# A hybrid decoder layer: gate tiles ahead of convolution tiles, and eight partial output products in the last recurrence

## The chip, the cores and the metric

The kernel runs on one core of a Trainium2 chip (trn2). The metric is the device time of one execution in microseconds (us); lower is better. The engines are called TensorE (PE in the profile; PEld is its weight load), VectorE (DVE), ScalarE (ACT), GpSimd (POOL) and SyncE (SP, which issues the transfers).

## The reference

One step of a one-layer decoder trunk. The input is 512 prompt tokens and 8 sequences of 8 sample tokens, 576 columns in all, of width 1024, in float32. With the two token mixers shortened to their names it reads:

```python
def token_mixers(hn, conv_buf, shift_buf, ssm0, wkv0, w):
    proj = hn @ w['w_in']
    z, xbc, dt_raw, rw = jnp.split(proj, IN_SPLITS, axis=-1)
...
    xbc_act = jax.nn.silu(conv)
    xs, bm, cm = jnp.split(xbc_act, XBC_SPLITS, axis=-1)
...
    y, ssm_fin = ssd_chunked(xs, dt, a_head, bm, cm,
...
    yg = (y.reshape(b, l, SSD_WIDTH) * jax.nn.silu(z.astype(f32))).reshape(b, l, SSD_GROUPS, SSD_WIDTH // SSD_GROUPS)
...
    o, wkv_fin = wkv_scan(rh, heads(decay), kh, vh, kk, heads(a), wkv0)
...
    y_rwkv = (on + bonus.reshape(b, l, RWKV_WIDTH)) * gate
    out = jnp.concatenate([y_ssd, y_rwkv], axis=-1).astype(dtype) @ w['w_out']

def layer(h, p, conv_buf, shift_buf, ssm0, wkv0, w):
    mix, conv_new, shift_new, ssm_new, wkv_new = token_mixers(
        rmsnorm(h, w['norm_mix']), conv_buf, shift_buf, ssm0, wkv0, w)
    h = h + mix
    hf = rmsnorm(h, w['norm_ffn'])
    h = h + (jax.nn.silu(hf @ w['w_gate']) * (hf @ w['w_up'])) @ w['w_down']
    gate = jax.nn.sigmoid(rmsnorm(h, w['norm_ple']) @ w['w_ple_gate'])
    h = h + gate * (p.astype(h.dtype) @ w['w_ple_proj'])
```

The combined projection gives 8 column tiles of 128 for the gate z, 12 for xBC (a causal convolution of 4 taps and SiLU follow), 16 columns of dt, and 26 tiles for RWKV-7 (r, k, v of 16 heads, and the low-rank inputs of decay, rate and gate). `ssd_chunked` is Mamba-2's recurrence in chunks of 128 tokens, `wkv_scan` the delta-rule recurrence of RWKV-7 with a 64x64 state for each head. The new states are outputs too.

## The kernel before

Activations lie transposed, channels on partitions and 576 token columns along them. A float32 product is made of three matmuls of split operands: high times high, high times low and low times high, each in two halves of 288 columns (`mm3`, L221 to L223). So a projection tile (1024 inputs, 128 outputs) is 48 matmuls. Each weight block of 128x512 is loaded by SP (`raw`), copied to its high part by ScalarE (`whi`) and its low part is made by VectorE and GpSimd in turns (`wlo`, L206); this is `wsplit`, called by `wload` and `linear` (L234). The blocks lie in one array in the order in which the program uses them.

**RWKV in quarters.** The 16 heads are worked in four quarters of four heads. Each needs six projection tiles with the token shift (`shifted`), then a preparation (`prep`: scan, exponentials, normalised keys; VectorE, ScalarE and GpSimd), the Gram matrices of nine windows of 64 tokens (`gram`, matmuls L613, masks L623), and the inverse of the triangular matrices: `solve`, some 60 small VectorE operations that follow each other (L667 to L677), and `combine`, which joins blocks on TensorE (L698, L712). Then comes `chain`: nine steps, one for each window, each of which needs the state of the one before. A step (`core` and what stands around it) has matmuls L789, a copy on VectorE (L792), matmuls L797, a second copy (L805), then the products for the state (L823) and four state updates on VectorE (L831). `head_norm` (L901, L902, L912) ends the quarter. The solves and chain steps leave TensorE idle unless other products fill it.

**The fill.** All projection tiles stand in one list, `todo`, made by `projections()`; `fill()` takes the first of it. A tile is of one of four kinds:

- the six of a quarter;
- a convolution tile (`conved`, "xbc"): after 48 matmuls ScalarE copies to `E`, GpSimd adds the old rows, VectorE does three multiply-adds of 128x600 (L395) and two products (L400, L401), and the result goes to memory;
- a gate tile (`zed`, "z"): two ScalarE operations and one on VectorE (L411, name `hz`), then to memory;
- `dts`, the 16 columns of dt.

The table `FP` tells how many tiles are taken at eight places of each quarter's preparation, gram and inverse, and `fill_for` takes tiles until the coming quarter has its six. The code's order is a wish only: the program is written within a TileContext that schedules all engines with a timeline model, so an instruction may go earlier or later on its engine. In the kernel before, the list is: six tiles of quarter 0; B and C of xBC (4 tiles) and dt; quarter 1; five X tiles; quarter 2; three X tiles; quarter 3; eight gate tiles.

**The last quarter.** After `chain(Q[3])` is written, the string `SEQ` orders what goes beside it, one letter for one thing: z is a gate tile, held back by `issue_after` to a marked matmul; s is the next step of the generator `ssd()` (Mamba's loads, decays, chunk states); p is the projection of the per-layer embedding (`ple_proj`); y loads the six RWKV output tiles of quarters 0 to 2; w is a partial output product, 36 matmuls over those six tiles, to which the layer's input is added and which goes to memory (`part_d`). `NPART` counts the w. After the head norm of quarter 3, the rest of `ssd()` is written (the loop over 8 sampled states, L1150 to L1167, and 8 pairs of heads, L1178 to L1205), and then eight residuals: output tile c takes two RWKV tiles (12 matmuls) and its partial sum when c is below `NPART`, else all eight (48 matmuls) and the layer's input. Line L1289 adds. Then come Mamba's part of the output product (`scaled`), the feed-forward part, the embedding gate and the last norm, which make up the time from 880 us on.

## Time and profile before

| | |
|---|---|
| time, median of 3 runs | 1346.01 us (1341.81 to 1350.75) |
| span of the profiled execution | 1349.0 us |
| mean granted TensorE clock | 0.940 |
| busy PE / DVE / ACT / POOL | 92% / 61% / 46% / 46% |
| moved | 135.58 MB, mean 100 GB/s |

The profile is of one execution; its span runs from the first to the last instruction. The busy share of an engine counts its instructions, not its waits; matmuls are pipelined and overlap, so that a busy TensorE may still be slowed, and the granted clock says at which share of its full speed it was let run. A table of windows gives, for a stretch of time, the busy time of each engine with the number of its instructions, the clock, the share of the transfer engines and the bytes moved. "A <- B" after an idle time is the engine and tile whose end released the waiting one.

### The profile page before, as it was taken

To read this page: it belongs to the slowest core of one execution; us is meant where nothing else is said; L and a number is where in the kernel's file an instruction comes from. 1 tells how busy PE (TensorE), PEld (TensorE's weight loads), DVE (VectorE), ACT (ScalarE), POOL (GpSimd) and SP (SyncE) were. 2 spreads that over 40 slices of the span, in tenths; PEclk is the share of its full clock that TensorE was granted. 3 is DMA by queue.
4 is the path that set the end of the run, shared out by engine and by line. 5 is a ranking of instruction groups with operands and counts; after the bars stand their busy time and mean duration, and the time that the engine had idled before them with its cause. 6 is when DMAs were issued, how large, how long until landed. Compare 5 with 4: busy or idle time off the path is not lost.

```text
span 1349.0 us, 26596 instructions
## 1 busy us (share of the span) xinstructions
PE 1246.8 (92%) x10525; PEld 1150.7 (85%) x10525; DVE 826.0 (61%) x1443; ACT 618.9 (46%) x1256; POOL 625.6 (46%) x597
## 2 busy tenths in 40 slices
PE   6897999999989978899999969989999999999997
PEld 6787897889868957788779859889999999999997
DVE  6648666887687785943466667886553135443454
ACT  6565436534654463343434364464442124433363
POOL 5425413642355154122456645565654336654642
PEclk9897799899979978889989989998999999999998
DMA  5322242234232412262454542222323222314322
GB/s 164 125 68 66 77 117 63 85 103 116 75 99 78 109 41 80 94 214 83 157 176 131 179 125 72 73 93 88 92 88 87 79 86 82 93 59 149 96 89 71
DMA packets 94461, 135.58 MB, mean 100 GB/s; under 512 B 34705, under 2 KB 39057, under 8 KB 94337
## 3 DMA queue, kind: packets, MB, share of 16 engines
q1 hardware_dynamic: 93760, 133.36, 32.4%
q8 instruction: 83, 1.36, 0.4%
q10 hardware_dynamic: 576, 0.52, 0.1%
q14 instruction: 42, 0.34, 0.1%
HBM read 106.10 MB, written 27.75 MB: 99 GB/s over the span
## 4 chain that ended last, share of the span: by engine, by line
PE 63%; DVE 14%; ACT 4%; issue 4%; DMA 3%; POOL 3%; DVEq 0%; SPq 0%; ACTq 0%; POOLq 0%
PE lin L234 21%; PE lin L1403 8%; PE lin L223 6%; PE lin L221 6%; PE lin L222 6%; DVE h L395 2%; PE lin L1508 1%; PE lin L1509 1%; PE lin L1510 1%; DVE tmp L674 1%; DVE wlo L206 1%; DVE Tt L676 1%; PE lin L613 1%; PE cx L797 1%; DVE suv L831 1%
## 5 line engine op out<-in xcount | busy, mean ns | idle before, releaser
L206 POOL TENSOR_TENSOR wlo<-raw,whi 128x512 fp32r<-128x512 f32 (+1 forms) x108 | 146.4, 1356 | 352.5 <-ACT whi L93 269.5
L93 ACT ACTIVATE whi<-raw 128x512 fp32r<-128x512 f32 (+1 forms) x232 | 143.3, 618 | 259.1 <-PE lin L234 126.4
L221 PE MATMUL lin<-xhi,whi 128*128 128x288 f32 (+1 forms) x784 | 243.3, 311 | 2.5 <-ACT whi L93 2.2
L223 PE MATMUL lin<-xhi,wlo 128*128 128x288 f32 (+1 forms) x784 | 241.5, 308 | 2.3 <-POOL wlo L206 2.3
L222 PE MATMUL lin<-xlo,whi 128*128 128x288 f32 (+1 forms) x784 | 241.5, 308 | 0.3 <-POOL xlo L194 0.3
L206 DVE TENSOR_TENSOR wlo<-raw,whi 128x512 fp32r<-128x512 f32 (+1 forms) x124 | 100.9, 814 | 103.2 <-PE lin L234 60.4
L221 PEld LDWEIGHTS lin<-xhi,whi 128*128 128x128 f32 (+1 forms) x784 | 151.0, 193 | 9.3 <-ACT whi L93 2.6
L223 PEld LDWEIGHTS lin<-xhi,wlo 128*128 128x128 f32 (+1 forms) x784 | 150.7, 192 | 6.2 <-POOL wlo L206 2.8
L222 PEld LDWEIGHTS lin<-xlo,whi 128*128 128x128 f32 (+1 forms) x784 | 150.8, 192 | 4.8 <-issue 1.2
L234 PE MATMUL lin<-xhi,whi 128*128 128x288 f32 x384 | 62.3, 297 | 3.2 <-ACT xhi L93 3.0
L234 PE MATMUL lin<-xlo,whi 128*128 128x288 f32 x384 | 60.8, 298 | 0.0
L234 PE MATMUL lin<-xhi,wlo 128*128 128x288 f32 x384 | 59.3, 297 | 0.0
L234 PEld LDWEIGHTS lin<-xhi,whi 128*128 128x128 f32 x384 | 54.6, 189 | 3.8 <-ACT xhi L93 1.7
L234 PEld LDWEIGHTS lin<-xlo,whi 128*128 128x128 f32 x384 | 54.8, 191 | 0.0
L234 PE MATMUL lin<-ah,wlo 128*128 128x288 f32 x352 | 54.7, 296 | 0.0
L234 PE MATMUL lin<-al,whi 128*128 128x288 f32 x352 | 54.7, 296 | 0.0
L234 PE MATMUL lin<-ah,whi 128*128 128x288 f32 x352 | 54.7, 296 | 0.0
L234 PEld LDWEIGHTS lin<-xhi,wlo 128*128 128x128 f32 x384 | 54.3, 191 | 0.0
L1403 PE MATMUL lin<-T,wh 128*128 128x288 f32 x320 | 50.1, 296 | 4.5 <-DVE T L194 2.8
L674 DVE TENSOR_TENSOR tmp<-L,Tt 72x30 f32<-72x30 f32 (+14 forms) x120 | 49.2, 410 | 3.2
L234 PEld LDWEIGHTS lin<-ah,whi 128*128 128x128 f32 x352 | 49.6, 189 | 0.0
L234 PEld LDWEIGHTS lin<-ah,wlo 128*128 128x128 f32 x352 | 49.6, 189 | 0.0
(425 smaller groups left out, 3197.8 us busy)
## 6 DMA issues: line engine op xcount, KB each, us to landing
raw<-wts SPq DMA_DIRECT2D x271, 256.0 KB, 2.6
S<-s_wkv SPq DMA_DIRECT2D x8, 512.0 KB, 5.1
hd<-s_ssm SPq DMA_DIRECT2D x8, 512.0 KB, 4.5
o_ssm_s<-hd SPq DMA_DIRECT2D x8, 512.0 KB, 2.9
xbc_d<-E SPq DMA_DIRECT2D x12, 288.0 KB, 2.1
x<-xT SPq DMA_DIRECT2D x8, 288.0 KB
gate_d<-g SPq DMA_DIRECT2D x8, 288.0 KB, 2.5
bv_d<-rw SPq DMA_DIRECT2D x8, 288.0 KB
```

The costliest lines, as they stand in the source:

```text
L93: return S.activation(out, in_, func, bias=bias, scale=scale)
L206: eng.tensor_tensor(lo[:, 0:n], raw[:, 0:n], hi[:, 0:n].bitcast(F32), ALU.subtract)
L221: T.matmul(ps[:, a:b], whi, xhi[:, a:b], start=first, stop=False)
L222: T.matmul(ps[:, a:b], whi, xlo[:, a:b], start=False, stop=False)
L223: T.matmul(ps[:, a:b], wlo, xhi[:, a:b], start=False, stop=last)
L234: T.matmul(ps[:, a:e], (hi, lo)[p][:, i * P:(i + 1) * P], xs[k + i][q][:, a:e], start=n == k + i == 0, stop=n == 2 and k + i == nk - 1, sk ...
L395: V.scalar_tensor_tensor(h[:], E[:, i:i + 600], w(i), h[:], ALU.mult, ALU.add)
L613: T.matmul(ps[:, c:c + 128].rearrange("p (a t) -> p a t", a=2), s.BK[jj][H[e], g].rearrange("p a t -> p (a t)"), s.G[H[e], g, jj, :, e], s ...
L674: V.tensor_tensor(o, L[:, jx:jx + 1, jx + 1:32].to_broadcast([NB, jx, n]), Tt[:, 0:jx, jx:jx + 1].to_broadcast([NB, jx, n]), ALU.mult)
L676: V.tensor_tensor(Tt[:, 0:jx, jx + 1:32], Tt[:, 0:jx, jx + 1:32], o, ALU.subtract)
L797: T.matmul(uw[H[e], jj, :], TT[H[e], g, jj, :], xs[H[e], jj, :], start=True, stop=True)
L1403: T.matmul(ps, (hi, lo)[p][:, k * P:(k + 1) * P], OPS[n][k][q], start=first and p == q == k == 0, stop=p == 1 and k == 3, skip_group_check ...
```

## The change

Five edits. `projections()` gives each of quarters 1 to 3 four convolution tiles right behind its own six tiles, and puts two "light" tiles (gate tiles, at the end one gate tile and dt) behind each quarter's; the list is then: six of quarter 0, z0, z1; six of quarter 1, B and C, z2, z3; six of quarter 2, X0 to X3, z4, dt; six of quarter 3, X4 to X7; z5, z6, z7. `FP` takes two tiles in each preparation instead of three, and `fill_for` goes on until no convolution tile heads the list, so that the four are written after the quarter's six and before its preparation. `SEQ` has no z: the embedding's projection comes first, and eight partial output products stand between and behind Mamba's steps, so `NPART` is 8 and every residual is the short one with 12 matmuls. The marks for the gate tiles go.

```diff
-SEQ = "zzszszszspyw"
+SEQ = "psyswswswwwwww"
...
-FILL = (5, 5, 3, 0)
-FP = ((1, 0, 1, 0, 1, 0, 0, 0), (1, 0, 1, 0, 1, 0, 0, 0), (1, 0, 1, 0, 1, 0, 0, 0), (0, 0, 0, 0, 0, 0, 0, 3))
+FP = ((1, 0, 1, 0, 0, 0, 0, 0), (1, 0, 1, 0, 0, 0, 0, 0), (1, 0, 1, 0, 0, 0, 0, 0), (0, 0, 0, 0, 0, 0, 0, 3))
...
-    rest = [("xbc", c) for c in CONV_BC] + [("dt", 0)] + [("xbc", c) for c in CONV_X] + [("z", c) for c in range(8)]
+    conv = [("xbc", c) for c in CONV_BC + CONV_X]
+    light = [("z", c) for c in range(5)] + [("dt", 0)]
     out = []
     for q in range(4):
         out += [(q, c) for c in in_tiles(q)]
-        out += rest[:FILL[q]]
-        rest = rest[FILL[q]:]
-    return out + rest
+        if q:
+            out += conv[:4]
+            conv = conv[4:]
+        out += light[:2]
+        light = light[2:]
+    return out + [("z", c) for c in range(5, 8)]
...
     def fill_for(s):
-        while len(s.t) < 6:
+        while len(s.t) < 6 or todo[0][0] == "xbc":
             fill()
...
-    while todo and todo[0][0] != "z":
-        fill()
+    assert all(what == "z" for what, _ in todo)
...
-    places = [("n", 2), ("c", 3), (3, 1), (3, 2), (3, 3)]
     for what in SEQ:
-        if what == "z":
-            with tc.issue_after(marks[places.pop(0)].ins):
-                fill()
-        elif what == "s":
+        if what == "s":
             next(steps)
```

What stands where is seen in the instruction order of each engine. The line numbers of the changed kernel are higher by 3 in its middle part and lower by 2 in the part from the SSD loop on.

VectorE in the preparation of the first quarter. Before (`h` and `E` are a convolution tile's, `kk`, `bk`, `lo`, `pb` the preparation's, `wlo` a weight split):

```order
L579 SCALAR_TENSOR_TENSOR kk_1131<-lo_1118,kk_1131 128x576
L395 SCALAR_TENSOR_TENSOR h_1087<-E_1079,hw,h_1087 128x600
L584 SCALAR_TENSOR_TENSOR bk_1145<-kk_1131,lo_1108 64x9x64 x2
L395 SCALAR_TENSOR_TENSOR h_1087<-E_1079,hw,h_1087 128x600
L581 TENSOR_TENSOR lo_1118<-lo_1118,rw_532 128x576
L395 SCALAR_TENSOR_TENSOR h_1087<-E_1079,hw,h_1087 128x600
L561 SCALAR_TENSOR_TENSOR lo_1245<-rmask,lo_1245 128x576
L206 TENSOR_TENSOR wlo_1297<-raw_1294,whi_1296 128x512
L400 SCALAR_TENSOR_TENSOR E_1079<-th_1092,h_1087 128x512
L401 SCALAR_TENSOR_TENSOR E_1079<-th_1092,h_1087 128x64
L565 TENSOR_TENSOR ar_981<-rw_834,pb_1258 128x576
```

And now (`hz` is a gate tile's):

```order
L579 TENSOR_TENSOR pb_1113<-kk_1123,pb_1113 128x576
L414 SCALAR_TENSOR_TENSOR hz_1083<-thz_1085,hz_1083 128x576
L582 SCALAR_TENSOR_TENSOR kk_1123<-lo_1110,kk_1123 128x576
L587 SCALAR_TENSOR_TENSOR bk_1137<-kk_1123,lo_1100 64x9x64 x2
L584 TENSOR_TENSOR lo_1110<-lo_1110,rw_539 128x576
L564 SCALAR_TENSOR_TENSOR lo_1222<-rmask,lo_1222 128x576
L209 TENSOR_TENSOR wlo_2031<-raw_2028,whi_2030 128x512
L568 TENSOR_TENSOR ar_988<-rw_841,pb_1235 128x576
L521 COPY rx_1246<-rn_1089 128x512
```

The convolution's multiply-adds between the preparation's steps are gone, and one operation of a gate tile stands in their place.

VectorE at the first chain steps of the third quarter. `TT` is the joined inverse, `xs` and `suv` are the two copies and the state updates of a chain step. Before:

```order
L719 COPY TT_465<-cx_5055 32x16x32
L581 TENSOR_TENSOR lo_6023<-lo_6023,rw_5621 128x576
L792 COPY xs_5111<-cx_5108 64x128
L561 SCALAR_TENSOR_TENSOR lo_6068<-rmask,lo_6068 128x576
L565 TENSOR_TENSOR ar_5968<-rw_5825,pb_6081 128x576
L805 TENSOR_SCALAR suv_5090<-cx_5114 64x2x64
L518 COPY rx_6092<-rn_6002 128x512
L595 SCALAR_TENSOR_TENSOR lo_6023<-rw_5757,pv,lo_6023 128x576
L831 SCALAR_TENSOR_TENSOR suv_5131<-suv_5090,pc_4410,cx_5126 64x64 x4
L574 SCALAR_TENSOR_TENSOR kk_6091<-rw_5689,pv,cb_6096 128x448
L792 COPY xs_5151<-cx_5148 64x128
```

And now:

```order
L722 COPY TT_472<-cx_5069 32x16x32
L795 COPY xs_5125<-cx_5122 64x128
L209 TENSOR_TENSOR wlo_6098<-raw_6095,whi_6097 128x512
L398 SCALAR_TENSOR_TENSOR h_6054<-E_6046,hw,h_6054 128x600
L808 TENSOR_SCALAR suv_5104<-cx_5128 64x2x64
L398 SCALAR_TENSOR_TENSOR h_6054<-E_6046,hw,h_6054 128x600 x2
L403 SCALAR_TENSOR_TENSOR E_6046<-th_6059,h_6054 128x512
L404 SCALAR_TENSOR_TENSOR E_6046<-th_6059,h_6054 128x64
L834 SCALAR_TENSOR_TENSOR suv_5145<-suv_5104,pc_4540,cx_5140 64x64 x4
L209 TENSOR_TENSOR wlo_6180<-raw_6177,whi_6179 128x512
L398 SCALAR_TENSOR_TENSOR h_6136<-E_6128,hw,h_6136 128x600
L795 COPY xs_5165<-cx_5162 64x128
```

What stood between the steps was the next quarter's preparation; now it is convolution tiles and weight splits, and that preparation comes later.

VectorE ahead of the SSD loop (`h` with the operand `lin` is a residual's add, `xdt` and `hin` are Mamba's chunk inputs and states). Before:

```order
L1289 TENSOR_TENSOR h_8706<-lin_8687,yl_8707 128x576
L206 TENSOR_TENSOR wlo_8744<-raw_8741,whi_8743 128x512
L1087 TENSOR_TENSOR xdt_7868<-d_7870,tk_7182 128x512
L1087 TENSOR_TENSOR xdt_7868<-d_7877,tk_7182 128x512
L1289 TENSOR_TENSOR h_8771<-lin_8710,yl_8772 128x576
L206 TENSOR_TENSOR wlo_8809<-raw_8806,whi_8808 128x512
L1102 TENSOR_TENSOR hin_7884<-hin_7884,d_7885 128x512
L1102 TENSOR_TENSOR hin_7884<-hin_7884,d_7889 128x512
L1087 TENSOR_TENSOR xdt_7893<-d_7895,tk_7182 64x512
L1087 TENSOR_TENSOR xdt_7893<-d_7902,tk_7182 64x512
L1289 TENSOR_TENSOR h_8836<-lin_8775,yl_8837 128x576
L206 TENSOR_TENSOR wlo_8874<-raw_8871,whi_8873 128x512
```

And now:

```order
L1287 TENSOR_TENSOR h_9084<-lin_9065,yl_9085 128x576
L1089 TENSOR_TENSOR xdt_8246<-d_8255,tk_7554 128x512
L1287 TENSOR_TENSOR h_9107<-lin_9088,yl_9108 128x576
L1287 TENSOR_TENSOR h_9130<-lin_9111,yl_9131 128x576
L209 TENSOR_TENSOR wlo_9161<-raw_9158,whi_9160 128x256
L1287 TENSOR_TENSOR h_9153<-lin_9134,yl_9154 128x576
L1104 TENSOR_TENSOR hin_8262<-hin_8262,d_8263 128x512
L1287 TENSOR_TENSOR h_9176<-lin_9157,yl_9177 128x576
L209 TENSOR_TENSOR wlo_9207<-raw_9204,whi_9206 128x256
L1104 TENSOR_TENSOR hin_8262<-hin_8262,d_8267 128x512
L1287 TENSOR_TENSOR h_9199<-lin_9180,yl_9200 128x576
L1089 TENSOR_TENSOR xdt_8271<-d_8273,tk_7554 64x512
```

The adds stood apart, each behind its own 48 matmuls and 128x512 splits, and five of the eight inside the loop's work; now all eight stand close together, each behind 12 matmuls and a 128x256 split.

## The prediction

> **What bounds the kernel now.** I read the page's head first, then busy time by stage, then durations of single forms, and last the waits in the stages that the change touches.
>
> ```profile
> span 1349.0 us, 26596 instructions
> PE 1246.8 (92%) x10525; PEld 1150.7 (85%) x10525; DVE 826.0 (61%) x1443; ACT 618.9 (46%) x1256; POOL 625.6 (46%) x597
> ```
>
> TensorE is busy for 92% of the span, so one would look for fewer matmuls. The change takes none away; it only puts them elsewhere. So what counts is where TensorE does not run at its rate. The next rows cut the span at the landmarks of the work: the end of gram of each quarter (139.5, 268.6, 409.2, 526.7), the first chain step of each quarter (201.3, 348.6, 485.0, 595.8), the first residual (697.3), the first sampled step of the SSD loop (722.0) and its end. The columns are: window, length, busy PE, PEld, DVE, ACT, POOL, granted clock, DMA share, GB/s. Two rows of the timeline show how such landmarks were found, the last block of gram and the first step of the chain.
>
> ```profile
> 137.30 2.08 PE L613 MATMUL lin<-G,bk 64*128 64x128 f32 x16 [0.52 <-ACT G L93]
> 201.32 0.71 PE L789 MATMUL cx<-suv,G 128*128 128x128 f32 x4
> ```
>
> ```profile
> 0.00:139.50 139.50, 110.73 (x814) 103.94 (x815) 89.58 (x134) 81.71 (x147) 63.07 (x95) 0.89 0.32 102
> 139.50:201.30 61.80, 58.61 (x509) 54.33 (x509) 43.04 (x97) 22.53 (x47) 18.43 (x19) 0.92 0.38 104
> 201.30:268.60 67.30, 62.02 (x577) 51.59 (x575) 48.43 (x86) 41.97 (x91) 33.90 (x45) 0.90 0.25 75
> 268.60:348.60 80.00, 77.51 (x783) 72.18 (x783) 60.66 (x140) 32.84 (x79) 26.99 (x31) 0.98 0.39 110
> 348.60:409.20 60.60, 55.12 (x501) 45.57 (x496) 49.51 (x82) 37.67 (x80) 31.22 (x42) 0.83 0.23 74
> 409.20:485.00 75.80, 69.49 (x712) 62.43 (x712) 58.14 (x141) 35.00 (x82) 23.77 (x26) 0.97 0.34 95
> 485.00:526.70 41.70, 33.01 (x335) 24.74 (x334) 28.25 (x56) 20.25 (x49) 20.56 (x23) 0.77 0.15 47
> 526.70:595.80 69.10, 60.84 (x571) 52.42 (x569) 48.39 (x120) 24.75 (x55) 17.09 (x20) 0.85 0.39 111
> 595.80:697.30 101.50, 96.97 (x808) 78.19 (x805) 46.75 (x106) 45.56 (x105) 38.41 (x33) 0.95 0.49 163
> 697.30:722.00 24.70, 24.70 (x196) 23.46 (x195) 16.61 (x25) 9.94 (x18) 13.19 (x11) 1.00 0.37 111
> 722.00:796.00 74.00, 68.05 (x658) 57.75 (x656) 46.37 (x90) 33.06 (x90) 46.25 (x40) 0.93 0.52 169
> 796.00:880.00 84.00, 74.75 (x650) 72.06 (x651) 61.21 (x66) 40.50 (x71) 46.29 (x27) 1.00 0.26 80
> 880.00:1349.00 469.00, 454.95 (x3444) 452.03 (x3442) 229.04 (x310) 193.10 (x348) 246.47 (x189) 0.98 0.29 88
> ```
>
> The reader is to see two kinds of stage. From 880 on, and from 697.3 to 722.0, TensorE is full at a clock near 1.00: nothing moves there but by its own count of matmuls. In the stages from a chain step to the end of gram (0.90, 0.83, 0.77) and in the first preparation TensorE is short of work, VectorE carries 70 to 85% of the time, and what is issued in between sets the end. There the DVE work that is added or removed is the price. The rate of TensorE with nothing in its way is this row:
>
> ```profile
> 1050.00:1100.00 50.00, 50.00 (x378) 50.00 (x377) 10.54 (x14) 10.79 (x18) 20.49 (x15) 1.00 0.28 81
> ```
>
> 50.0 / 378 = 0.132 us for a matmul of 128x288, so a projection tile of 48 matmuls is 6.35 us, a partial product of 36 is 4.8 us, and a residual of 12 is 1.6 us.
>
> **The change, part by part.** Prices on VectorE, one form in each row (busy, then mean ns):
>
> ```profile
> L395 DVE SCALAR_TENSOR_TENSOR h<-E,hw,h 128x600 f32<-128x600 f32 x36 | 36.7, 1018 | 4.7 <-ACT h L93 4.3
> L831 DVE SCALAR_TENSOR_TENSOR suv<-suv,pc,cx 64x64 f32<-64x64 f32 x112 | 31.3, 280 | 13.7 <-PE cx L823 11.2
> L400 DVE SCALAR_TENSOR_TENSOR E<-th,h 128x512 f32<-128x512 f32 x12 | 11.3, 939 | 0.0
> L805 DVE TENSOR_SCALAR suv<-cx 64x128 f32<-64x128 f32 x36 | 10.6, 294 | 14.0 <-ACT suv L93 13.1
> L792 DVE COPY xs<-cx 64x128 f32<-64x128 f32 x36 | 10.6, 294 | 15.4 <-ACT xs L93 14.8
> L401 DVE SCALAR_TENSOR_TENSOR E<-th,h 128x64 f32<-128x64 f32 x12 | 5.2, 435 | 0.0
> L411 DVE SCALAR_TENSOR_TENSOR hz<-thz,hz 128x576 f32<-128x576 f32 x8 | 6.1, 766 | 5.1 <-ACT thz L93 5.1
> ```
>
> A convolution tile costs VectorE 3 x 1.018 + 0.939 + 0.435 = 4.43 us, a gate tile 0.77, a chain step 0.294 + 0.294 + 4 x 0.280 = 1.71. On TensorE the two kinds of tile are alike. Now by stage, with counts from the instruction order before and after.
>
> *First preparation, to 139.5.* Three convolution tiles go, two gate tiles come: 3 x 4.43 - 2 x 0.77 = 11.8 us less on VectorE. Its own windows in the middle of it:
>
> ```profile
> 120.00:130.00 10.00, 5.76 (x76) 4.93 (x73) 9.74 (x11) 4.22 (x9) 6.98 (x8) 0.60 0.21 61
> 130.00:140.00 10.00, 7.91 (x60) 6.96 (x59) 4.92 (x12) 5.28 (x14) 8.28 (x15) 0.50 0.09 31
> ```
>
> VectorE is full until 130 and TensorE waits for it at half rate, so nearly all of it comes out: **-11** (bounds -5, if the ACT and POOL chain of gram then ends last, to -12).
>
> *First solve, to 201.3.* One convolution tile less among the solve's serial VectorE steps (4.43): **-3.5** (0, if projections on TensorE, 58.6 of 61.8 busy, end last, to -4.4).
>
> *First chain to second gram, 201.3 to 268.6.* One convolution tile, two gate tiles and one chain step more ahead of the last gram: 4.43 + 1.54 + 1.71 = +7.7 on a VectorE that has 67.3 - 48.4 = 18.9 us free. I take somewhat over half: **+4.5** (0 to +7.7).
>
> *Second solve to chain, 268.6 to 348.6.* Two convolution tiles and a chain step go from VectorE (10.6), and TensorE has about 6.3 projection tiles ahead of the matmuls that join the inverse instead of 8 (1.7 x 6.35 = 10.8). Both lie on the same stretch, so they don't add up wholly: **-14** (-8 to -18).
>
> *Second chain to third gram, 348.6 to 409.2.* One convolution tile, a gate tile, dt and three chain steps come in: 4.43 + 0.77 + 5.1 + about 1 = +11.5, and the stretch had 60.6 - 49.5 = 11.1 free. Since its VectorE mostly waits on steps that follow each other, little of it is free for a tile that stands between two steps: **+11** (+5 to +12). So the two stages together win 3 us: what the solve gives up, the chain gets.
>
> *Third gram to fourth gram, 409.2 to 526.7.* Here four convolution tiles come where none was ahead of gram: 4 x 4.43 = 17.7. Two chain steps more stand ahead of it (3.4). And the next preparation, of which a good part (18 us of VectorE by the order) was done before the first chain step at 485.0, now lies behind it: that shortens one stage and lengthens the next. Net +21 on VectorE against 41.7 - 28.3 = 13.4 free in the second of them. TensorE gets two more tiles of fill, 12.7 us, where its clock was 0.77, which hides them. I take **+18.5** (+8 to +25), nearer the full price since the order puts whole convolution tiles between a step's matmuls and its copies.
>
> *Fourth solve to chain, 526.7 to 595.8.* The head norm's VectorE copies move into the solve and three gate tiles stay; some 84 matmuls of the per-layer embedding (84 x 0.132 = 11 us) come ahead of the join, where the clock was 0.85 and TensorE 60.8 of 69.1 busy: they fit. **-5** (-8 to +3).
>
> *Last chain, 595.8 to 697.3.* Five gate tiles go (31.7 us), seven partial products come (33.6 us), the embedding goes before it. Seven more loads of 288 KB, as many stores, seven VectorE adds lie beside TensorE's 97 of 101.5 us and VectorE's 46.8. **-3** (-8 to +6, if the loads of x and of split weights come late).
>
> *Residual, 697.3 to 722.0.* All eight residuals, 12 matmuls each (12.7 us), stand together ahead of the loop; before, three stood here, one short and two of 48, among 196 matmuls. Each now reads 288 KB of partial sums, two buffers deep: **-3** (-8 to +4).
>
> *SSD loop, 722.0 to 796.0.* Residual tiles of 48 matmuls were its fill:
>
> ```profile
> L221 PE MATMUL lin<-xhi,whi 128*128 128x288 f32 x64 | 19.1, 299 | 0.0
> ```
>
> With the two other products that is 192 matmuls, four tiles, 25.3 us at 0.132. VectorE's waits there say what it costs to stand behind them:
>
> ```profile
> DVE yoff L1157 <- PE d L1153: 5.4, 5, 2.1
> DVE hd L1166 <- PE d L1165: 3.6, 4, 1.7
> DVE hd L1166 <- POOL hd L1161: 3.2, 5, 1.4
> DVE xs L1205 <- PE y L1204: 3.1, 3, 1.4
> DVE h L1289 <- PE lin L223: 2.6, 3, 1.5
> ```
>
> Waits on TensorE are 14.7 us; POOL's 3.2 stay. Each sampled state is loaded, updated and stored in one of two buffers:
>
> ```profile
> hd<-s_ssm SPq DMA_DIRECT2D x8, 512.0 KB, 4.5
> o_ssm_s<-hd SPq DMA_DIRECT2D x8, 512.0 KB, 2.9
> ```
>
> Load and store alone hold a buffer 7.4 us, 3.7 per state, and POOL's own 46 us are left, so the loop can't come below about 54. I take **-10** (-20 to 0).
>
> The rest of the program keeps its order: 0. The sum: -11 - 3.5 + 4.5 - 14 + 11 + 18.5 - 5 - 3 - 3 - 10 = **-15.5**. The profiled span of 1349.0 becomes 1333.5; it stands 3.0 us over the median of the runs shown (1346.01), so by the same ratio, 0.9978, the time is **1330.5 us**.
>
> **Rivals.** (1) *Chain steps that follow whole tiles, slower.* The interval between two chain steps is what TensorE has between them plus the round trip through VectorE:
>
> ```profile
> 290.30:305.00 14.70, 14.70 (x127) 13.77 (x126) 14.32 (x32) 5.92 (x12) 5.59 (x8) 1.00 0.26 77
> 510.00:515.50 5.50, 4.70 (x60) 3.60 (x59) 4.73 (x14) 3.21 (x11) 2.14 (x4) 1.00 0.27 101
> ```
>
> A step with little fill takes 5.5 us (second row); the stretch of the first row, 127 matmuls, has a full TensorE and a full VectorE at once. If a projection tile between two steps adds its matmuls (6.35) to its VectorE time, since the step's copies wait behind the one and its products behind the other, the first stage that begins with a chain step pays 7.7 + 6.35 = 14 where I had 4.5, the second 11.5 + 6.35 = 18 where I had 11, and the third 21 + 4 x 6.35 less the 41.7 x (1 - 0.77) = 9.6 us that TensorE's clock leaves free, 37 where I had 18.5. That is 35 us more: a sum of +19.5, 1368.5 in the trace, **1365 us**. For it: the clocks of 0.83 and 0.77 say that round trips, not TensorE's work, set these stages, and the changed order has convolution rows between a step's two copies. Against it: VectorE has 11 to 19 us free there. The kernel is slower than before once the three terms together pass 49.5 us (34 in my sum).
>
> (2) *The loop without fill gains nothing, no change.* TensorE's own work in the loop is 68.05 - 25.3 = 42.7 us at a clock of 0.93. Where TensorE was short of work its clock was 0.50 and 0.60 (the two rows of the first preparation). At 0.60 it is 42.7 x 0.93 / 0.60 = 66 us, and with the waits on POOL the loop stands at 72 or so; the residual stage likewise keeps its length. Then 13 of the 15.5 us are lost: 1346.5 in the trace, **1343.5 us**. For it: the loop's work comes in short pieces. Against it: 43 us of work in 60 is busier than those windows. [...]
>
> (3) *The free time of VectorE takes the convolutions, a larger gain.* With the two chain stages at +1 and +5 and the third at +10, the sum is -33: **1313 us**. For it: the 43 us that are free in the three stages together. Against: those are waits inside chains.
>
> (4) *That the change does not do it* can be left out: in the order printed for the changed kernel the gate tiles stand in the preparations, and eight short residuals together.
>
> **How the numbers follow.** My sum, 0.33, with (3) at 0.12 makes faster; (2), with the sum's own middling outcomes, 0.33; (1) 0.22. A measurement of this kernel tells about 1% from no change, that is 1332.5 and 1359.5; my forecast is barely over that bound, so much of its own spread falls into "same". Faster 0.45, same 0.33, slower 0.22. The range: the low end takes three terms at their better bounds (third to fourth gram +8, loop -20, last chain -8, that is 25 us less), 1305; the high end takes five sixths of what sets rival (1) apart from the sum, 1360.
>
> **What the changed profile would show.** The first gram should end near 128 instead of 139.5, with no L395-type work in 100 to 130. The stage from the third to the fourth gram should be 130 to 140 us instead of 117.5, the last chain of equal length, and the loop about 64 us between first sampled step and end, with VectorE's waits on TensorE nearly gone. Wrong would be: a clock near 0.6 in the loop with its length unchanged (rival 2), or growth over 49.5 us in the three stages from a chain step to gram (rival 1).

## The result and the profile after

The changed kernel takes 1394.79 us (median of 4 runs, 1392.91 to 1400.74) against 1343.91 us (4 runs, 1339.56 to 1350.75) for the kernel before on the same chips: a ratio of 1.0378, 95% interval 1.0338 to 1.0417. It is 51 us slower; the forecast was 1330.5 us, 15.5 us faster than the 1346.01 us known then. The head of its page shows no more work than before: as many matmuls (10525), and VectorE is busy for less time.

```profile
span 1391.0 us, 26671 instructions
PE 1273.4 (92%) x10525; PEld 1167.4 (84%) x10525; DVE 823.7 (59%) x1453; ACT 628.0 (45%) x1266; POOL 613.8 (44%) x601
```

The windows of the changed kernel, cut at the same landmarks as before (columns as there). The last three are cut otherwise than in the prediction, which ended the loop at 796.0, ahead of its last products: the loop up to the last products of the head pairs, the time from there to the first feed-forward product (the first that reads `XF`), and the rest:

```profile
0.00:129.80 129.80, 102.78 (x765) 95.34 (x765) 77.09 (x119) 76.67 (x137) 55.85 (x82) 0.89 0.33 105
129.80:187.30 57.50, 54.52 (x501) 52.21 (x501) 40.57 (x93) 17.64 (x42) 16.89 (x14) 0.94 0.39 105
187.30:270.00 82.70, 79.77 (x671) 66.90 (x667) 54.31 (x98) 50.57 (x106) 33.62 (x53) 0.88 0.25 82
270.00:335.80 65.80, 63.41 (x642) 59.48 (x640) 48.55 (x122) 25.09 (x61) 21.70 (x20) 0.97 0.41 108
335.80:424.50 88.70, 82.70 (x736) 68.13 (x732) 59.84 (x105) 55.68 (x113) 35.72 (x52) 0.85 0.25 78
424.50:491.50 67.00, 62.82 (x618) 58.75 (x616) 48.79 (x116) 24.38 (x58) 21.60 (x20) 0.95 0.36 99
491.50:570.70 79.20, 71.74 (x620) 58.61 (x616) 54.45 (x101) 46.69 (x97) 31.20 (x45) 0.78 0.25 75
570.70:642.20 71.50, 55.81 (x524) 49.12 (x522) 51.95 (x116) 25.19 (x51) 21.65 (x25) 0.90 0.50 141
642.20:748.10 105.90, 99.31 (x797) 80.40 (x797) 48.64 (x105) 37.44 (x93) 31.05 (x32) 0.89 0.47 149
748.10:773.50 25.40, 16.57 (x123) 14.65 (x123) 17.66 (x28) 8.95 (x17) 12.35 (x12) 0.89 0.53 158
773.50:854.50 81.00, 64.43 (x572) 50.49 (x572) 44.87 (x86) 37.58 (x100) 46.91 (x40) 0.74 0.36 121
854.50:904.90 50.40, 49.40 (x398) 48.32 (x399) 41.02 (x48) 21.40 (x38) 29.54 (x18) 1.00 0.23 74
904.90:1391.00 486.10, 470.15 (x3587) 465.04 (x3587) 235.99 (x319) 200.72 (x361) 255.74 (x195) 0.99 0.30 89
```

The kernel before, cut at the same landmarks (its feed-forward part begins at 862.3 us):

```profile
722.00:812.10 90.10, 79.55 (x783) 67.93 (x781) 56.87 (x102) 46.24 (x115) 53.77 (x45) 0.94 0.48 154
812.10:862.30 50.20, 47.20 (x383) 46.44 (x382) 40.56 (x45) 20.47 (x34) 30.75 (x19) 1.00 0.22 65
862.30:1349.00 486.70, 470.99 (x3587) 467.46 (x3587) 239.21 (x319) 199.95 (x360) 254.49 (x194) 0.98 0.29 89
```

The reader is to see the third, fifth and seventh rows: the stages from a chain step to the end of gram are 82.7, 88.7 and 79.2 us long where they were 67.3, 60.6 and 41.7. All of the loss stands before the first residual: 748.1 against 697.3 is 50.8 us. Some 9 us come back behind it, in the loop, which is 9 us shorter although its clock is 0.74 where it was 0.94; the two stretches after the loop are as long as they were. So the two traces are 42.0 us apart.

The same landmarks for the kernels that the next section speaks of, each from its profiled execution, in us from the stage's start to its end (loop and tail are the first two of the three windows above):

| stage | before | changed | list_only | parts_only | spread_conv | parts4 | spread_list |
|---|---|---|---|---|---|---|---|
| to gram 0 | 139.4 | 129.8 | 131.0 | 138.4 | 130.3 | 130.3 | 129.6 |
| solve 0 to chain 0 | 61.9 | 57.5 | 56.3 | 60.7 | 56.9 | 57.6 | 58.6 |
| chain 0 to gram 1 | 67.2 | 82.7 | 80.1 | 67.3 | 79.7 | 82.7 | 78.2 |
| solve 1 to chain 1 | 80.1 | 65.8 | 66.4 | 80.1 | 65.0 | 65.6 | 65.3 |
| chain 1 to gram 2 | 60.5 | 88.7 | 87.9 | 60.5 | 80.3 | 88.9 | 81.9 |
| solve 2 to chain 2 | 75.8 | 67.0 | 66.3 | 75.9 | 64.8 | 67.2 | 62.8 |
| chain 2 to gram 3 | 41.7 | 79.2 | 79.2 | 38.0 | 70.7 | 79.2 | 69.6 |
| solve 3 to chain 3 | 69.1 | 71.4 | 70.2 | 67.7 | 72.5 | 71.4 | 71.5 |
| chain 3 to residuals | 101.5 | 106.0 | 76.7 | 135.8 | 110.4 | 91.1 | 79.3 |
| residuals to loop | 24.7 | 25.3 | 26.7 | 19.7 | 25.1 | 23.1 | 27.7 |
| loop | 90.2 | 81.0 | 85.1 | 73.8 | 83.1 | 74.8 | 87.2 |
| tail | 50.1 | 50.4 | 50.5 | 52.2 | 48.6 | 51.8 | 50.7 |
| the rest | 486.8 | 486.0 | 483.3 | 483.1 | 487.1 | 485.4 | 483.1 |

The rest holds the same work in all of them and still runs from 483.1 to 487.1 us, and the stage from chain 2 to gram 3 is 41.7 or 38.0 us with the same list of tiles (before, parts_only): differences of 4 us between two traces say little.

What the three long stages gained is fill on TensorE. One row of each kernel, the third of the three matmuls of a split product, in the stage from chain 1 to gram 2, before:

```profile
L223 PE MATMUL lin<-xhi,wlo 128*128 128x288 f32 x43 | 13.1, 304 | 0.0
```

and changed:

```profile
L226 PE MATMUL lin<-xhi,wlo 128*128 128x288 f32 (+1 forms) x82 | 24.9, 303 | 0.0
```

Counted so over all split products, the three stages hold 185, 151 and 0 matmuls before and 266, 268 and 180 now; the two stages from gram to the chain that follow the first and the second hold 401 and 312 before and 332 and 324 now. At 0.132 us the additions are 10.7, 15.4 and 23.8 us; the stages grew by 15.4, 28.1 and 37.5, so the added matmuls alone don't make up the growth.

And where in the stage they stand (two windows of the changed kernel, one from the first chain step on and one at the end with gram; then the largest groups of TensorE in that end):

```profile
336.00:375.00 39.00, 39.00 (x337) 32.73 (x337) 26.91 (x40) 23.67 (x46) 17.33 (x24) 1.00 0.38 116
404.00:424.50 20.50, 20.50 (x200) 17.12 (x196) 10.70 (x26) 9.72 (x26) 9.96 (x15) 0.54 0.10 31
```

```profile
L616 PE MATMUL lin<-G,bk 64*128 64x128 f32 x64 | 8.6, 407 | 0.0
L737 PE MATMUL cb<-G,S 64*64 64x16 f32 x64 | 4.9, 266 | 0.0
```

First 39 us with a full TensorE at full clock, which hold two thirds of the stage's split products, and at the end 20.5 us at 0.54 with gram, the states and chain steps. The kernel before has such an end too,

```profile
391.00:409.20 18.20, 17.55 (x207) 15.07 (x206) 13.93 (x31) 10.59 (x27) 9.21 (x13) 0.61 0.05 18
```

so the low clock there is not new. In the stage from chain 2 to gram 3, which grew most, the changed kernel's parts are

```profile
491.50:530.00 38.50, 36.59 (x301) 30.62 (x297) 24.56 (x38) 23.39 (x45) 15.58 (x23) 1.00 0.38 112
530.00:550.00 20.00, 14.79 (x99) 10.71 (x100) 16.00 (x31) 14.01 (x28) 8.37 (x11) 0.55 0.14 50
550.00:570.70 20.70, 20.36 (x225) 17.29 (x223) 13.89 (x34) 9.28 (x25) 7.26 (x11) 0.61 0.10 29
```

The last two, 40.7 us, are about as long as the whole stage was (41.7). The projections stand in one heap ahead, and what they could have lain beside stands behind them.

### The profile page after: what moved, and what is told of

The parts are those of the page before. It is cut to its first block, busy times and chain, and to the rows that moved or that the text cites. A ratio compares the mean times of both kernels' runs of the same rounds, so it can differ in the third digit from the quotient of the medians.

```text
span 1391.0 us, 26671 instructions
## 1 busy us (share of the span) xinstructions
PE 1273.4 (92%) x10525; PEld 1167.4 (84%) x10525; DVE 823.7 (59%) x1453; ACT 628.0 (45%) x1266; POOL 613.8 (44%) x601
## 4 chain that ended last, share of the span: by engine, by line
PE 65%; DVE 16%; DMA 7%; ACT 5%; issue 4%; POOL 2%; SPq 0%; DVEq 0%; ACTq 0%; POOLq 0%
PE lin L237 21%; PE lin L1401 7%; PE lin L224 7%; PE lin L226 7%; PE lin L225 7%; PE lin L616 2%; DMA o_ssm_s<-hd 1%; DVE wlo L209 1%; PE cx L792 1%; DMA raw<-wts 1%; DVE tmp L677 1%; PE cx L800 1%; PE cx L815 1%; DMA yl<-part_d 1%; DVE Tt L679 1%
## 5 line engine op out<-in xcount | busy, mean ns | idle before, releaser
L224 PEld LDWEIGHTS lin<-xhi,whi 128*128 128x128 f32 (+1 forms) x784 | 149.2, 191 | 10.7 <-ACT whi L96 3.0
L237 PE MATMUL lin<-xhi,whi 128*128 128x288 f32 x384 | 60.5, 297 | 0.3 <-ACT xhi L96 0.2
L237 PE MATMUL lin<-xhi,wlo 128*128 128x288 f32 x384 | 60.6, 295 | 0.0
L1401 PE MATMUL lin<-T,wh 128*128 128x288 f32 x320 | 51.8, 299 | 5.3 <-ACT T L96 1.8
L1401 PEld LDWEIGHTS lin<-T,wh 128*128 128x128 f32 x320 | 45.4, 189 | 6.9 <-ACT T L96 2.3
L237 PEld LDWEIGHTS lin<-al,whi 128*128 128x128 f32 x352 | 49.7, 189 | 0.0
```

The source lines that it names most:

```text
L224: T.matmul(ps[:, a:b], whi, xhi[:, a:b], start=first, stop=False)
L237: T.matmul(ps[:, a:e], (hi, lo)[p][:, i * P:(i + 1) * P], xs[k + i][q][:, a:e], start=n == k + i == 0, stop=n == 2 and k + i == nk - 1, sk ...
L1401: T.matmul(ps, (hi, lo)[p][:, k * P:(k + 1) * P], OPS[n][k][q], start=first and p == q == k == 0, stop=p == 1 and k == 3, skip_group_check ...
```

## The experiments

Three theories for the loss, on record before the first four kernels ran: A, the matmuls of the convolution tiles ahead of gram; B, the partial products; C, the convolution's VectorE operations between the chain steps.

**The list alone.** The changed kernel with one partial product:

```diff
-SEQ = "psyswswswwwwww"
+SEQ = "sssspyw"
```

> The changed list of tiles and its fill rules, but with one partial output product as before (the residuals of 48 matmuls are back beside the SSD loop) and no gate tile in the last chain. Theory A (TensorE: the four convolution tiles behind each quarter's six stand ahead of gram as 25 us of matmuls, and what they leave is a starved end of the stage): the first chain step of the last quarter stays at about 642 us, the last chain shrinks from 106 to 75-80 us, the residuals and the loop take about what they took before (99); 1355-1365 us. Theory B (the partial products are what costs): back to 1345-1350. Theory C (VectorE's part of the convolution tiles costs): the last quarter's first step at 642 as in A, the total as in A.

Measured: 1363.15 us, ratio 1.0166 (1.0124 to 1.0208). The last chain took 76.7 us, as A and C said; B alone falls.

**The products alone.** The kernel before with eight partial products behind its gate tiles:

```diff
-SEQ = "zzszszszspyw"
+SEQ = "zzszszszspywwwwwwww"
```

> The list of tiles before, with eight partial products in the last chain behind the five gate tiles. All theories: first step of the last chain at about 596 as before. Theory A and C: the last chain, already full on TensorE, grows by the 33 us of the seven products, and the loop without its fill gives back 5 to 10 of them, with a clock near 0.75: 1365-1375 us. Theory B: about what the change measured, 1385-1395. If the loop gave back in full what it loses in fill: 1345.

Measured: 1365.00 us, ratio 1.0185 (1.0133 to 1.0236). The last chain grew by 34.3 us, seven products at their full 4.8, and residuals, loop and tail together fell from 165.0 to 145.7, by 19.3; theories A and C had 5 to 10. The loop without its fill took 73.8 us at a clock of 0.79. So by the ratios the list costs 22 us (0.0166 x 1343) and the products 25 (18 to 32), and 22 + 25 = 47 of the 51: the change has two losses that add up. In the traces these stages show 15 of the 25; the profiled run was this kernel's fastest, 1355.31 us.

**VectorE's part of the convolution.** The changed kernel without taps 1 to 3:

```diff
-        for i in range(1, 4):
-            V.scalar_tensor_tensor(h[:], E[:, i:i + 600], w(i), h[:], ALU.mult, ALU.add)
```

> The changed kernel without the three multiply-adds on VectorE in each of the twelve convolution tiles (36.7 us of VectorE in all; the convolution's taps 1 to 3 are left out). Theory A: TensorE's matmuls ahead of gram set the stages, so 5 to 12 us are won: 1383-1390. Theory C: these operations between the chain steps are what lengthens the three stages, 25 to 35 us are won: 1360-1370.

Measured: 1394.85 us, ratio 1.0383 (1.0329 to 1.0436): nothing is won by taking 36.7 us off VectorE. The stage from chain 1 to gram 2 has VectorE at 44.5 us instead of 59.8 and is as long as it was (88.5 against 88.7):

```profile
336.10:424.60 88.50, 83.97 (x738) 69.48 (x734) 44.49 (x92) 55.19 (x112) 32.75 (x53) 0.85 0.24 78
```

C falls.

**TensorE's part.** The changed kernel with half of each convolution tile's matmuls:

```diff
+                if part == 0 or i < part:
+                    mm3(ps, hi[:, i * P:(i + 1) * P], lo[:, i * P:(i + 1) * P], xh, xl, k + i == 0,
+                        k + i == (nk - 1 if part == 0 else nk - 5 + part))
...
-        linear(X, ps)
+        linear(X, ps, part=2)
...
```

> The changed kernel with 24 instead of 48 matmuls in each of the twelve convolution tiles (the second two inputs of each weight block are left out; loads and splits stay): 12 x 24 x 0.132 = 38 us less on TensorE. Theory A: the stages from a chain step to gram end 8 to 12 us earlier each, 25-35 us in all: 1360-1370. Theory C: TensorE has slack there, under 10 us are won: 1385-1392.

Measured: 1375.71 us, ratio 1.0271 (1.0217 to 1.0324); 0.0107 x 1343 = 14 us less than the changed kernel for 38 us of matmuls, with intervals that leave 5 to 23. The same stage is 9.2 us shorter (79.5). TensorE's part counts and VectorE's does not, but A's 25 to 35 were too much: more than half of what is taken away only leaves a gap.

**The place.** The same tiles in the same quarters, but taken one by one inside the preparation:

```diff
-FP = ((1, 0, 1, 0, 0, 0, 0, 0), (1, 0, 1, 0, 0, 0, 0, 0), (1, 0, 1, 0, 0, 0, 0, 0), (0, 0, 0, 0, 0, 0, 0, 3))
+FP = ((1, 0, 1, 0, 0, 0, 0, 0), (2, 1, 1, 1, 1, 0, 0, 0), (2, 1, 1, 1, 1, 0, 0, 0), (2, 1, 1, 0, 0, 0, 0, 3))
...
-        while len(s.t) < 6 or todo[0][0] == "xbc":
+        while len(s.t) < 6:
```

> The changed kernel with the same tiles in the same quarters, but the four convolution tiles and the two light ones taken one by one within the preparation (fill table rows 2 1 1 1 1) instead of four ahead of it. Theory A1 (the place: what stands ahead of the preparation delays it, and the preparation and gram then run with an empty TensorE at half clock): gram of quarters 1 to 3 ends 8 to 15 us earlier each, 20-35 us won in all, 1358-1375 us. Theory A2 (the amount: five gate tiles and the embedding are simply more TensorE work than these stages can hide): under 8 us won, 1385-1395.

Measured: 1371.71 us, ratio 1.0205 (1.0164 to 1.0247), 0.0173 x 1343 = 23 us won. The three stages hold 288, 288 and 192 matmuls of split products, more than the changed kernel's 266, 268 and 180, and are shorter by 3.0, 8.4 and 8.5 us. The stage from chain 1 to gram 2 and its end, which had a clock of 0.54:

```profile
331.90:412.20 80.30, 76.32 (x703) 63.74 (x698) 55.59 (x97) 48.87 (x103) 34.76 (x50) 0.91 0.25 79
...
392.00:412.20 20.20, 19.72 (x244) 15.46 (x242) 9.81 (x25) 11.49 (x28) 10.44 (x15) 0.83 0.13 43
```

So A holds in its narrower form A1: the place, four tiles in a heap ahead of the preparation, costs some 23 us. The tiles themselves are still paid where they stand now: the three stages hold 103, 137 and 192 more matmuls of split products than before, 13.6, 18.1 and 25.3 us at 0.132, and are 12.5, 19.8 and 29.0 us longer than before. The place was not tried by itself on the old list: the kernel before with its convolution tiles written ahead of the preparation (before_ahead, expected at 1353 to 1363 us if the place costs by itself) deadlocks and gave no time.

**Both losses undone.** spread_conv with one partial product, so that of the change only the new order of the tiles stays, gate tiles early and convolution tiles later:

```diff
-SEQ = "psyswswswwwwww"
+SEQ = "sssspyw"
```

> The changed list with the convolution tiles taken one by one in the preparations, and one partial product: both costly parts of the change undone, what stays is gate tiles ahead of convolution tiles. If the parts add up (list +22, of which place 22, products +24): 1335-1347 us, as before. If gate tiles in the early quarters cost by themselves (more TensorE work in stages with a half clock): 1350-1360.

Measured: 1348.18 us, ratio 1.0036 (1.0016 to 1.0057). Place and products make up 46 of the 51 us; the new order by itself costs some 5 (2 to 8), although the first chain step comes 13 us earlier (188.3 against 201.3).

**How many products.** The changed kernel with four:

```diff
-SEQ = "psyswswswwwwww"
+SEQ = "psyswswsww"
```

> The changed kernel with four partial products in the last chain instead of eight; four residuals of 48 matmuls stand by the SSD loop again. If each product costs the same (24 us for seven): 1378-1384 us. If the loop's gaps hold only the first few tiles: 1371-1376. If the products cost only beyond four, 1370 or less.

Measured: 1370.14 us, ratio 1.0194 (1.0158 to 1.0231). The first three products cost 0.0028 x 1343 = 4 us over list_only, the last four 0.0184 x 1343 = 25. From the first step of the last chain to the first feed-forward product, list_only, parts4 and the changed kernel do the same matmuls in another order (the products in the chain or in the residuals). Their rows, in this order, are

```profile
637.50:876.40 238.90, 220.10 (x1886) 188.16 (x1885) 150.04 (x255) 105.48 (x242) 124.29 (x97) 0.91 0.37 123
```

```profile
642.90:883.60 240.70, 219.87 (x1887) 187.18 (x1885) 150.33 (x260) 104.48 (x243) 121.92 (x98) 0.91 0.40 130
```

```profile
642.20:904.90 262.70, 229.71 (x1885) 193.86 (x1885) 152.19 (x266) 105.38 (x247) 119.86 (x100) 0.87 0.40 127
```

So the first three products cost 1.8 us and the last four 22.0, near the ratios' 4 and 25. The chain takes 14.4 us more for the first three, their full price, and 14.9 more for the last four. Behind the chain the first three win 12.7 us back; with the last four it is 7.2 us longer again, although 144 matmuls fewer stand there. The loop alone had clocks of 0.92, 0.89 and 0.74 (the last is in the windows of the changed kernel above):

```profile
740.80:825.90 85.10, 77.90 (x756) 66.92 (x752) 53.23 (x97) 44.11 (x112) 51.50 (x43) 0.92 0.45 152
```

```profile
757.10:831.90 74.80, 66.14 (x648) 54.47 (x647) 48.83 (x92) 40.18 (x105) 48.90 (x41) 0.89 0.48 160
```

Missing fill alone does not make the 81.0 us, since the loop of parts_only has none either and takes 73.8. Why the loop grows with the last four is not shown.

**Fill for the empty loop.** The changed kernel with 24 matmuls that no one reads in each sampled step, paced by that step's mask `bm`:

```diff
+        jk = mt("jk", [P, 8])
...
+            jp = lin_ps()
+            for i in range(24):
+                T.matmul(jp[:, 0:256], YR[7][0][:, 0:P], bm[:, i % 2], start=True, stop=True)
+            V.tensor_copy(jk[:], jp[:, 0:8])
```

> The changed kernel with 24 more matmuls of 128x256 (about 2.8 us) in each of the eight sampled steps of the SSD loop, whose result no one reads: about 22 us of TensorE work in place of the residual tiles' 25. Theory L1 (clock: without fill TensorE is held at 0.74, and its short matmuls then set the pace): the clock in the loop goes to 0.9 or more and the 81 us of the loop shrink to 70-77 although work was added. Theory L2 (transfers, POOL and waits set the pace): the work goes into gaps, 79-84 us at whatever clock. Theory L3 (TensorE's time adds up): 90-105 us.

Measured: 1387.60 us, ratio 1.0330 (1.0288 to 1.0371), not slower than the changed kernel's 1.0338 to 1.0417 and perhaps faster. Seven of the eight residuals moved into the loop's end as well, so its length can't be set against 81.0; from the last chain's first step to the first feed-forward product it is 257.1 against 262.7 us. The loop ran at 0.93:

```profile
761.90:848.40 86.50, 82.64 (x822) 72.17 (x822) 55.87 (x108) 44.30 (x114) 52.02 (x44) 0.93 0.45 154
```

The eight sampled steps alone can be compared. They hold 144 of the 192 added matmuls (48 went ahead of the first step) and one residual's 12. First the changed kernel, then this one:

```profile
773.50:826.80 53.30, 40.70 (x416) 31.22 (x415) 27.10 (x66) 19.24 (x55) 32.04 (x30) 0.76 0.37 129
761.90:814.00 52.10, 51.24 (x563) 44.49 (x562) 28.70 (x72) 17.49 (x51) 30.09 (x28) 0.92 0.36 133
```

L3 falls: the 192 matmuls are some 22 us (an estimate, 192 x 0.132 x 256 / 288), and the 144 of them that stand in these steps cost nothing there (52.1 against 53.3 us). The steps are as long at a clock of 0.92 as at 0.76, which speaks for L2 and its gaps: TensorE's idle time went from 12.6 to 0.9 us, and in the changed kernel its largest wait there was for the loads of the states (7.3 us). L1 is not excluded, since the added work may have used up what the higher clock gave.

**Fill for the end of gram.** The changed kernel with 12 matmuls behind each of gram's five groups in quarters 1 to 3:

```diff
+            if s.q:
+                with tc.issue_after(gm.ins):
+                    jp = cb_ps()
+                    for i in range(12):
+                        T.matmul(jp[:, 0:HALF], X[0][0][:, 0:P], X[1][0][:, 0:HALF], start=True, stop=True)
+                    V.tensor_copy(jk[:], jp[:, 0:8])
...
```

> The changed kernel with 12 more matmuls of 128x288, whose result no one reads, behind each of the five groups of gram in quarters 1 to 3: 180 matmuls, 23.8 us of TensorE at its full rate, into a stretch where TensorE is busy all the time at a clock of 0.50 to 0.56. Theory G1 (half clock: gram's and the states' small matmuls fill TensorE's time but do not lift its clock, large ones do): the clock there rises to 0.8 or more and the extra work is paid back, 1385-1402 us against 1395. Theory G2 (TensorE's time adds up): 1412-1420.

Measured: 1398.45 us, ratio 1.0405 (1.0368 to 1.0442): 4 us more than the changed kernel for 23.8 us of work, with intervals that overlap, within G1's numbers. But the clock at the end of gram rose only to 0.68 in the stage from chain 1,

```profile
400.00:427.00 27.00, 25.48 (x221) 21.63 (x223) 12.23 (x31) 12.86 (x32) 10.48 (x19) 0.68 0.08 24
```

and in the stage from chain 2 it was 0.62 (545.0 to 576.0) where it had been 0.61. The three stages grew by 4.1, 6.3 and 8.3 us. Of these 18.7 us 6.3 came back in the two solves that follow and 3.3 in the last chain, so G1's reason is hardly borne out.

**A tile in gram.** The kernel before with each preparation's third convolution tile held until gram's third group:

```diff
-FP = ((1, 0, 1, 0, 1, 0, 0, 0), (1, 0, 1, 0, 1, 0, 0, 0), (1, 0, 1, 0, 1, 0, 0, 0), (0, 0, 0, 0, 0, 0, 0, 3))
+FP = ((1, 0, 1, 0, 0, 0, 1, 0), (1, 0, 1, 0, 0, 0, 1, 0), (1, 0, 1, 0, 0, 0, 1, 0), (0, 0, 0, 0, 0, 0, 0, 3))
...
+                with tc.issue_after(pin[0]) if pin[0] else nullcontext():
+                    mm3(ps, hi[:, i * P:(i + 1) * P], lo[:, i * P:(i + 1) * P], xh, xl, k + i == 0, k + i == nk - 1)
...
+                pin[0] = gm.ins
                 fill_at(s, 5 if gs[0] == 0 else 6)
+                pin[0] = None
```

> The kernel before with the third convolution tile of each preparation of quarters 0 to 2 held back until the matmuls of gram's third group and put between them and the fourth. Theory G1: the 48 matmuls lift the clock in gram and come out of the full stretch ahead, 1 to 3 us a quarter: 1333-1340 us against 1342.5. Theory G2: 6.35 us are moved from one place to another of the same stage, and the chain steps that follow wait: 1342-1350.

Measured: 1369.47 us, ratio 1.0194 (1.0162 to 1.0227), worse than either theory. In the first quarter the tile was only moved: gram's third group ended 6.0 us earlier (129.1 against 135.0), the tile's 48 matmuls came next, and gram ended where it had (139.7 against 139.4). The loss came later: 5.5 us in the first solve, 9.5 in the stage from chain 1 to gram 2, and 9.7 in the stage from chain 2 to gram 3, which has no tile in its gram; the solves between gave 3.1 and 6.9 back. The rows of gram's matmuls over all four quarters, before

```profile
L613 PE MATMUL lin<-G,bk 64*128 64x128 f32 x288 | 36.8, 378 | 6.8 <-POOL bk L585 2.9 <-ACT G L93 2.5 <-ACT E L93 1.4
```

and with the tile in gram:

```profile
L615 PE MATMUL lin<-G,bk 64*128 64x128 f32 x288 | 40.7, 382 | 11.5 <-POOL bk L587 10.9 <-ACT G L93 0.3
```

TensorE idles 11.5 us ahead of gram's matmuls instead of 6.8, most of it for GpSimd's keys `bk`. G1's numbers fall; why the later stages grew so much is not shown.

**Small doses.** The kernel before with one gate tile of the last chain moved into the last preparation, and with one moved beside the last solve:

```diff
-SEQ = "zzszszszspyw"
+SEQ = "zszszszspyw"
...
-(0, 0, 0, 0, 0, 0, 0, 3)
+(0, 0, 1, 0, 0, 0, 0, 3)
...
```

> The kernel before with one gate tile of the last chain taken in the last quarter's preparation instead, where the clock was 0.77: the change in its smallest dose. Theory A1: the tile (6.35 us) falls on a stage that has that much free, if it stands within the preparation: that stage grows by 0 to 3 us, the last chain shrinks by 5 to 6; 1336-1341 us against 1341. Theory A2: the stage grows by the tile's whole 6 us, no change or slower, 1341-1345.

Measured: 1342.94 us, ratio 0.9998 (0.9980 to 1.0016). The preparation's stage did not grow (38.0 us, as in parts_only, which has no tile there), and the last chain did not shrink (104.7 against 101.5), though it holds a tile less.

```diff
-SEQ = "zzszszszspyw"
+SEQ = "zszszszspyw"
...
-(0, 0, 0, 0, 0, 0, 0, 3)
+(0, 0, 0, 0, 0, 0, 0, 4)
...
```

> The kernel before with one gate tile of the last chain taken beside the last solve instead (four there, not three), where the clock was 0.85. Theory A1 and A2: VectorE's solve sets that stage's length and TensorE has about 10 us free beside it; the stage grows by 0 to 3 us (the join of the inverse waits behind the tile), the last chain shrinks by 5 to 6; 1336-1341 us against 1341.

Measured: 1350.45 us, ratio 1.0058 (1.0032 to 1.0083). The solve's stage was 70.2 and the last chain 107.8 us, longer with less in it. Both kernels also drop the first of the five marks that hold gate tiles back, which may be why; this was not tried apart.

**Early gate tiles with the rest in place.** Two gate tiles in the first preparation, convolution tiles inside the later ones (mix), or spread as before (mix3), three gate tiles in the last chain (the list, `FP` and `SEQ` change with `FILL`):

```diff
-FILL = (5, 5, 3, 0)
+FILL = (2, 4, 5, 4)
...
```

> Gate tiles 0 and 1 in the first preparation, four, four (with dt) and four convolution tiles one by one inside the preparations of quarters 1 to 3, three gate tiles beside the last solve, three in the last chain, one partial product. If the early gate tiles keep their 14 us and the later quarters lose less than that, having three tiles fewer than the changed list: 1332-1340 us. If the convolution tiles moved to later quarters cost there what was won ahead: 1342-1350.

Measured: 1370.94 us, ratio 1.0194 (1.0158 to 1.0229).

```diff
-FILL = (5, 5, 3, 0)
+FILL = (4, 5, 4, 2)
...
```

> As mix, but with the convolution tiles spread as in the kernel before (two left for the time ahead of quarter 1's six tiles, three within each preparation, the rest ahead of the next quarter's six): 1332-1340 us if the gain ahead is kept, 1342-1350 if it is paid back.

Measured: 1352.25 us, ratio 1.0065 (1.0045 to 1.0086). In both the gain ahead is there at the first chain step (187.0 and 193.9 against 201.3) and is gone later: in mix at the last quarter's first chain step (615.5 against 595.8), in mix3 at the first residual (705.8 against 697.3). None of these kernels beats the one before.

## Why the prediction was wrong

The forecast was faster by 15.5 us in the trace; the trace has 42.0 more. By its own steps, in order:

- *First preparation* -11: measured -9.6. *First solve* -3.5: -4.4. Both right. The reason given for the first, three convolution tiles less on VectorE, was not tried by itself.
- *First chain to second gram* +4.5: measured +15.4. *Second chain to third gram* +11: +28.1. *Third gram to fourth gram* +18.5: -8.8 and +37.5, so +28.7. **This is the step that failed.** It was mis-sized by 38 us in all, and the price was taken on the wrong engine. I read TensorE as short of work in these stages and VectorE as what sets their end, so I costed a convolution tile there by its 4.43 us on VectorE against the time that VectorE had free. The rows that I read it from say otherwise: TensorE was busy for 92, 91 and 79% of the three stages, VectorE for 72, 82 and 68%. For the third stage I set the matmuls down as hidden, "two more tiles of fill, 12.7 us, where its clock was 0.77, which hides them". The count by stage gives 192 matmuls more from the third to the fourth gram, four tiles and 25.3 us, and 180 of them stand in the stage from chain 2 to gram 3. The runs showed the reverse of my price: without most of that VectorE work the time stays the same (no_conv_vec), with half of the convolution tiles' matmuls it falls by 14 us (half_conv_mm), and with the same tiles spread, not in a heap, by 23 (spread_conv). A mean clock of 0.77 hid nothing: TensorE is nearly full at 1.00 for the 38.5 us of the heap (36.6 busy), and the stage's old length follows behind it. (In the second of them the sum 4.43 + 0.77 + 5.1 + 1 is 11.3, not 11.5, which changes nothing.) How the growth beyond the added matmuls (81.0 against 49.9 us in the three stages, of which 23.0 come back in the two solves between them) splits into parts is not shown.
- *Second solve to chain* -14: measured -14.2, right.
- *Fourth solve to chain* -5: measured +2.4, within its bounds. *Last chain* -3: measured +4.4, within its bounds, for the reason that stood there: five gate tiles and the embedding go, the seven products come.
- *Residual* -3: measured +0.7. *SSD loop* -10: measured -9.2, up to the last products of the head pairs; the window that the forecast was made for ended at 796.0, ahead of them. Behind the loop nothing changed (536.9 us before, 536.5 now), as forecast. So the gain expected of the short residuals came, all but the residual stage's 3.7 us.

The three stages' 38 us are most of the 57.5 us between forecast and trace; the fourth solve and the last chain, 7.4 us each, and the residual are most of what is left.

Of the rivals, the first gave 14, 18 and 37 for the three stages, 69 in all; measured are 15.4, 28.1 and 28.7, 72 in all. It stated the right mechanism in half (a tile's matmuls are paid in full there) and the wrong one in the other half (on top of its VectorE time), so the closeness of its 69 is partly luck. The time it gave was short by 22.5 us in the trace (1368.5 against 1391.0), since it kept my terms for the fourth solve, the last chain and the residual. The second, the loop without fill at a lower clock, came true in part: the clock fell, to 0.74 and not to 0.60, but the loop's length did not stay, it fell by 9.2 us. (My argument against it misread the rows: 43 us of work in 60 is 71%, and the window with a clock of 0.50 was busy for 79%.) What it warns of may be in the last four products, with which the loop grew from 74.8 us at 0.89 to 81.0 at 0.74 (parts4 and the changed kernel).

The range ended at 1360 because its high end took five sixths of the one rival and left the other terms at their middling values, and because the case of slower had a chance of only 0.22. Both rivals together, 1368.5 + 13 = 1381.5 us in the trace, would still have been short.

## What to carry to other kernels

When an order is changed on a kernel whose busiest engine is 92% full, count that engine's instructions by stage in both orders first, and price a stage by them; the mean clock of 0.77 in the stage from chain 2 to gram 3 was not room by itself. In a heap ahead of work that waits, the fill here cost more than its matmuls' time (81.0 us against 49.9 at 0.132 in the three stages), since the work behind it ran alone; a tile at a time it cost about that time (61.3 against 57.0). Moving three output products ahead of the residuals cost next to nothing (1.8 us) and four more cost 22 us, so try such a change in doses. The losses of two parts of this change added up (22 and 25 of the 51 us), so a range must take in the sum of rivals that don't exclude each other.

## What the runs showed of the hardware

At the end of gram in the changed kernel (404.0 to 424.5 us) TensorE's granted clock was 0.54 while its records show it busy for 20.50 of 20.50 us; the two largest groups there are float32 matmuls of 64x128 and 64x16 (407 and 266 ns each, rows L616 and L737 above). From 336.0 to 375.0 us it was as full, 39.00 of 39.00 us, and its clock was 1.00; 174 of its 337 matmuls there are split products of 128x288 (305 ns each). So here a TensorE that the records show full had both clocks, beside different matmuls; what made the difference is not shown. The busy time there is modelled, but no idle time stands before those two rows (0.0 in both). With large matmuls put among the small ones (junk_gram, 180 of 128x288 over three quarters) the clock was 0.68 instead of 0.54 in one quarter and 0.62 instead of 0.61 in the next, and the kernel's time was 1398.45 us against 1394.79, so they were no remedy here. In the sampled steps 144 additional matmuls of 128x256 (junk_loop), with one residual beside them, went with a clock of 0.92 instead of 0.76 and cost nothing that could be measured (52.1 us against 53.3).
